# Splitting the second token group's operand straight from the transposed input, with the norm's roots applied as panels leave PSUM, and one ring of raw buffers

## The chip, the cores and the metric

The kernel runs on one core of a Trainium2 chip. The metric is device microseconds of one execution; of the kernel before there are three timed runs, and their median is the time to beat. Beside them stands one profiled execution, from which every duration comes. The engines are PE (TensorE, matmul), ACT (ScalarE), DVE (VectorE), POOL (GpSimd) and SP (SyncE, which here issues most loads).

## The reference, cut to what matters

One layer of a streaming encoder: 1024 prompt frames and 128 sample frames (8 streams of 16), each of 2048 channels, all in f32.

```
h = x * rsqrt(mean(x*x, -1) + eps) * norm_pre
q_sb,k_sb,v_sb,gate_sb,q_r,k_r,v_r,gate_r = split(h @ w_in)       # 8 panels of 8 heads x 128
o_sb = stick_breaking(q_sb, k_sb, v_sb)      # prompt: causal; samples: over 1024 cached keys and values
o_r, state = retention(rope(q_r), rope(k_r), v_r)                  # chunks of 64
y = concat(head_rms(o_sb) * g * silu(gate_sb), head_rms(o_r) * g * silu(gate_r))
out = x + rms_norm(y @ w_out) * norm_post
```

The number that the change moves is the **root**, `rsqrt(mean(x*x) + eps)`, one per token. It is a factor of a whole row of `h`, so it can be multiplied into `x` ahead of the projection or into the panel `h @ w_in` behind it.

## The kernel before, in words

Tokens are worked in two groups. **Group 0** holds tiles 0 to 3 of the prompt and the sample tile (640 tokens, moved as pieces of 256 and 384); **group 1** holds tiles 4 to 7 (512 tokens, one piece). f32 products are made of three reduced ones: each operand is split into a high and a low part (ACT copies the high part, DVE subtracts: `split`, L165 to L168), and PE does high·high, high·low and low·high.

**The moving operand** of a group is `h` transposed, 16 blocks of 128 channels, kept as four quarters of four blocks (`mh`, `ml`). There is one such buffer, so group 1's quarter q overwrites group 0's.

**A panel** (`project`, L394) is 128 columns of `w_in`: four loads of weights `wr` of 256 KB, each split into `wh`, `wl` (two buffers each) and used in a block of 24 products in group 0 (12 in group 1). **Row products** (`project_rows`, L414) give v of two heads with tokens on partitions, from weights `wrn`.

**Prologue** (L508 to L627). Group 0's operand is split from the transposed input `x_cols` with only `norm_pre` applied (ACT L577, DVE L578) and the first two panels of retention head 0 follow it. ACT makes the squares of the rows (`mean_square`, L535); PE spreads the roots over partitions (L550), and group 0's panels are multiplied by them where they leave PSUM (`rooted`, L467, on DVE). Then come the row products of v, and `stage_rest` (L594), a job that is stepped between matmuls: it loads the rows of tiles 4 to 7, squares them, loads their part of `x_cols`, multiplies it by `norm_pre` and the roots (DVE L610) and stores it to the DRAM tensor `s_h` (4 MB). The gate panel of retention head 0 is computed beside it.

**Heads.** The loop at L1086 goes over groups and heads. Per head it computes panels for retention q (column 4), k (5), gate (7), and stick-breaking q (0), k (1), gate (3); the attention work of both branches runs as jobs that emit a piece after so many matmuls (`tick`). The order listings below show in what order each engine's rows stand.

**The change of groups.** With head 7 of group 0 the last two panels (columns 7 and 3) are made together by `project_pair` (L400): blocks 7.0, 3.0, 7.1, 3.1, 7.2, 3.2, 7.3, 3.3, where 3.1 is column 3 with quarter 1. Between them `load_moving` (L244) is stepped: each step splits one block of group 1's operand out of a raw buffer `mr` (read back from `s_h`) and asks for a later one. A split of quarter q waits until PE has done block 3.q. Weights `wr` and `wrn` share a ring of five raw buffers (tag "wr"); `mr`, `kpast` (old keys, re-read per head in group 1) and the left operands of the later phases share a ring of three (tag "mr").

**After the heads**, the output projection runs as a Strassen-like set of products of sums (`left`, `left_sample`, `product`), and its raw buffers come out of the same two rings.

Of the kernel before, what the change touches and what calls it, by code (L numbers as in the profile page):

```python
# [29 lines left out]
D_REST = 8  # L30
# [30 lines left out]
MR = 3  # L61
# [27 lines left out]
def tile_hybrid_step(  # L89
# [59 lines left out]
    roots = [const.tile([P, m], F32, name=f"root{i}") for i, (_, m) in enumerate(X_PIECES[:2])]  # L149
    root_of = const.tile([P, 5], F32, name="root_of")  # L150

    NB_TOK = GROUPS[1]["n"]
    s_h = scr.tile([P, KT, NB_TOK], F32, name="s_h")
# [10 lines left out]
    def split(hi, lo, src):  # L164
        return (  # L165
            nc.scalar.activation(hi, src, AF.Copy),  # L166
            nc.vector.tensor_tensor(lo, src, hi.bitcast(F32), ALU.subtract),  # L167
        )  # L168
# [75 lines left out]
    def load_moving(mov, at, n, src):  # L244
# [59 lines left out]
    def left(gi, n, hi, lo, bufs, tag, deep):  # L304
# [3 lines left out]
        def load(h):  # L308
            r = bufs.tile([P, 256], F32, name=tag, tag=tag, bufs=deep)
# [16 lines left out]
    def left_sample(kk, hi, lo, bufs, tag, deep):  # L326
        raw = []

        def load(h):
            r = bufs.tile([P, P], F32, name=tag, tag=tag, bufs=deep)  # L330
            pin(nc.sync.dma_start(r, s_y[0][kk * H + h][:, 4 * P : 5 * P]))
            raw.append(r)
# [81 lines left out]
    def project_rows(g, mov, col, dst, off, loads=None):  # L414
# [5 lines left out]
        for w in range(KT // 2):  # L420
            wr = wp.tile([P, 2, 2 * P], F32, name="wrn", tag="wr", bufs=5)
# [22 lines left out]
        for b, bank in enumerate(banks):  # L444
            m = min(2, nt - 2 * b)
            if phase[0] == 0:
                for i in range(m):
                    t = 2 * b + i
                    nc.scalar.activation(
                        dst[:, off + t].rearrange("p j d -> p (j d)"), bank[:, i, :], AF.Copy,  # L450
                        scale=root_of[:, t : t + 1],
                    )
                continue
            nc.scalar.activation(
                dst[:, off + 2 * b : off + 2 * b + m].rearrange("p t j d -> p t (j d)"), bank[:, :m, :], AF.Copy
            )

    with ExitStack() as s1:
# [3 lines left out]
        def evac_split(acc, hi, lo, off=0):  # L462
            for a, (o, m) in acc:
                m = min(m, NB_TOK - o)
                split(hi[:, off + o : off + o + m], lo[:, off + o : off + o + m], a[:, :m])

        def rooted(dst, a, i, m):  # L467
            nc.vector.tensor_tensor(dst, a[:, :m], roots[i][:, :m], ALU.mult)

        def gate(acc, tag):  # L470
            e = ep.tile([P, NMAX], F32, name=tag, tag=tag)
            for i, (a, (o, m)) in enumerate(acc):
                if phase[0] == 0:
                    rooted(e[:, o : o + m], a, i, m)
                    s = ep.tile([P, 512], F32, name="sw", tag="sw", bufs=1)
                    nc.scalar.activation(s[:, :m], e[:, o : o + m], AF.Sigmoid)
                    nc.vector.tensor_tensor(e[:, o : o + m], e[:, o : o + m], s[:, :m], ALU.mult)
                    continue
                nc.scalar.activation(e[:, o : o + m], a[:, :m], AF.Sigmoid)
                nc.vector.tensor_tensor(e[:, o : o + m], e[:, o : o + m], a[:, :m], ALU.mult)  # L480
# [17 lines left out]
        def ret_values(g, mov, h, loads=None):  # L498
            pair["r"] = ep.tile([P, 5, 2, P], F32, name="rv", tag="rv")
            project_rows(g, mov, col(6, h), pair["r"], 0, loads)  # L500
# [9 lines left out]
        with tc.tile_pool(name="p0", bufs=2) as p0, tc.tile_pool(name="p0s", bufs=1) as p0s, tc.tile_pool(  # L510
# [6 lines left out]
            pre = p0s.tile([P, KT], F32, name="pre")  # L517
            nc.sync.dma_start(pre, pre_cols)

            def load_x(t):  # L520
                halves = []
                for c in range(2):
                    xt = p0.tile([P, HALF], F32, name="xt", tag="xc0", bufs=4)
                    nc.sync.dma_start(xt, x_rows(t)[:, c * HALF : (c + 1) * HALF])
                    halves.append(xt)
                return halves

            def load_cols(piece, k, m):
                o, n = X_PIECES[piece]
                xc = p0.tile([P, m, n], F32, name=f"xc{piece}", tag=f"xc{piece % 2}", bufs=4)  # L530
# [4 lines left out]
            def mean_square(xt, ssq, i):  # L535
                for c, half in enumerate(xt):
                    pin(nc.scalar.activation(half, half, AF.Square, accum_out=ssq[:, c, i : i + 1]))
# [15 lines left out]
            def second_panel(w):  # L553
                wr = wp.tile([P, WQ, P], F32, name="wr", tag="wr", bufs=5)
# [16 lines left out]
            for piece, (o, m) in enumerate(X_PIECES[:2]):  # L571
                for w in range(KT // WQ):
                    xc = xcs[piece][w]
                    for j in range(WQ):
                        k = w * WQ + j
                        hi, lo = (half[w][:, j, o : o + m] for half in mov)
                        nc.scalar.activation(hi, xc[:, j, :], AF.Copy, scale=pre[:, k : k + 1])  # L577
                        nc.vector.scalar_tensor_tensor(  # L578
                            lo, xc[:, j, :], pre[:, k : k + 1], hi.bitcast(F32), ALU.mult, ALU.subtract
                        )  # L580
# [3 lines left out]
            ssq5 = p0s.tile([P, 2, len(tiles)], F32, name="ssq5")  # L584
            for i, t in enumerate(tiles):
                mean_square(load_x(t), ssq5, i)
# [7 lines left out]
            def stage_rest():  # L594
                rest = GROUPS[1]["tiles"]
                ssq = p0s.tile([P, 2, len(rest)], F32, name="ssq4")
                for i, t in enumerate(rest):
                    xt = load_x(t)
                    yield 6
                    mean_square(xt, ssq, i)  # L600
                    yield 4
                rb = p0s.tile([P, NB_TOK], F32, name="rb4")
                spread(rb, rows_of(ssq, "p4"), 0, last)
                yield 4
                for w in range(KT // 2):
                    xc = load_cols(2, 2 * w, 2)
                    yield 6
                    for j in range(2):
                        k = 2 * w + j
                        nc.vector.scalar_tensor_tensor(  # L610
                            xc[:, j, :], xc[:, j, :], pre[:, k : k + 1], rb, ALU.mult, ALU.mult
                        )
                        yield 4
# [3 lines left out]
            rstd = rows_of(ssq5, "p5")  # L617
            nc.vector.tensor_copy(root_of, rstd)
            for root, at in zip(roots, (0, 2)):
                spread(root, rstd, at, last)  # L620
            for table in (*first, *ropes):
                for i, (o, m) in enumerate(X_PIECES[:2]):
                    rooted(table[:, o : o + m], table[:, o : o + m], i, m)
# [970 lines left out]
```

## Time and profile before

| what | us |
|---|---|
| three timed runs: median (lowest to highest) | 2292.41 (2291.46 to 2292.89) |
| the profiled execution | 2297.38 |
| its span, in which every position below is counted | 2295.4 |
| PE busy in it | 2245.6 |
| DVE busy | 1254.0 |
| ACT busy | 918.2 |
| PE idle in it (span less busy) | 49.8 |

How to read it: the profile groups instructions by source line. "out<-in" names the tile written and the tile read; behind it stand the shape, the count, the busy time, the mean of one in ns, and the idle time of that engine just before such rows with what ended it. "PEclk" is the granted TensorE clock as a share of full speed. PE is busy nearly all the time, so the question is always where its few idle stretches lie, and at which clock it runs behind them.

### The profile page before, as it was taken

Reading aid. Unit: us, or ns where it says so; the run is one execution under the profiler, and the core shown is the slowest. Engines: PE = TensorE matmul, PEld = TensorE weight load, DVE = VectorE, ACT = ScalarE, POOL = GpSimd, SP = SyncE. Lnnn points to the kernel's source line nnn. Section 1 sums busy time; section 2 is a strip of 40 time slices with the busy share of each in tenths; the row PEclk is TensorE's granted clock in tenths of the full one; section 3 lists DMA queues with packets and bytes.
Section 4 is the critical chain, followed back from the end, with each engine's and each line's share of the span. In section 5 each row is a group of like instructions: output and inputs, shape, how many; then the busy total and the mean of one; then the engine's idle time right before and its main releaser. Section 6 shows DMA issues by size and latency. Waiting matters only on the chain.

```text
span 2295.4 us, 38963 instructions
## 1 busy us (share of the span) xinstructions
PE 2245.6 (98%) x14306; PEld 2028.6 (88%) x14306; DVE 1254.0 (55%) x2587; ACT 918.2 (40%) x1945; POOL 339.5 (15%) x577
## 2 busy tenths in 40 slices
PE   7899999999999999999999999999999999999998
PEld 7899999999999999998888889898889987888886
DVE  5435444454545545355556565656565567556567
ACT  7333333333333333334333333343443444545363
POOL 0002020110202020111202111120212212000020
PEclk9999999999999999999999999999999999999999
DMA  8947656675557648568669778788887767766586
GB/s 293 329 141 188 194 177 190 181 211 173 161 178 201 201 154 233 168 189 263 186 201 234 220 212 234 218 230 218 229 218 218 218 166 195 248 210 186 143 223 175
DMA packets 442848, 470.99 MB, mean 205 GB/s; under 512 B 182560, under 2 KB 302368, under 8 KB 442144
## 3 DMA queue, kind: packets, MB, share of 16 engines
q1 hardware_dynamic: 319408, 304.09, 46.8%
q0 software_dynamic: 28720, 78.41, 12.2%
q10 hardware_dynamic: 94528, 86.00, 11.8%
q8 instruction: 112, 1.84, 0.3%
q14 instruction: 80, 0.66, 0.1%
HBM read 363.51 MB, written 114.29 MB: 208 GB/s over the span
## 4 chain that ended last, share of the span: by engine, by line
PE 88%; DMA 6%; DVE 2%; ACT 2%; issue 1%; SPq 1%; DVEq 0%; ACTq 0%
PE acc L380 47%; PE accn L436 16%; PE a L1228 5%; PE a L1227 5%; PE a L1224 5%; PE pa L796 2%; PE z L766 2%; PE zc L835 1%; PE pd L899 1%; DMA ro<-s_rk 1%; DMA mr<-s_h 1%; DMA s_rk<-rk 1%; PE pa L944 1%; PE pS L959 1%; PE pa L949 1%
## 5 line engine op out<-in xcount | busy, mean ns | idle before, releaser
L380 PE MATMUL acc<-mh,wh 128*128 128x256 f32 (+2 forms) x2304 | 668.0, 341 | 7.3 <-ACT wh L166 7.3
L380 PE MATMUL acc<-mh,wl 128*128 128x256 f32 (+2 forms) x2304 | 660.6, 339 | 3.9 <-DVE wl L167 3.9
L380 PE MATMUL acc<-ml,wh 128*128 128x256 f32 (+2 forms) x2304 | 663.3, 340 | 0.0
L167 DVE TENSOR_TENSOR wl<-wr,wh 128x512 fp32r<-128x512 f32 x504 | 345.9, 689 | 418.9 <-ACT wh L166 396.6
L166 ACT ACTIVATE wh<-wr 128x512 fp32r<-128x512 f32 x504 | 317.0, 631 | 639.1 <-PE acc L380 336.9
L380 PEld LDWEIGHTS acc<-mh,wh 128*128 128x128 f32 x2304 | 422.0, 189 | 39.4 <-ACT wh L166 7.3
L380 PEld LDWEIGHTS acc<-mh,wl 128*128 128x128 f32 x2304 | 426.4, 189 | 32.1 <-DVE wl L167 4.4
L380 PEld LDWEIGHTS acc<-ml,wh 128*128 128x128 f32 x2304 | 423.8, 189 | 31.6 <-issue 3.3
L436 PE MATMUL accn<-whn,mh 128*128 128x256 f32 x1152 | 330.1, 287 | 7.6 <-ACT whn L166 7.6
L436 PE MATMUL accn<-wln,mh 128*128 128x256 f32 x1152 | 328.5, 285 | 0.0
L436 PE MATMUL accn<-whn,ml 128*128 128x256 f32 x1152 | 328.3, 285 | 0.0
L436 PEld LDWEIGHTS accn<-whn,mh 128*128 128x128 f32 x1152 | 222.6, 194 | 10.6 <-ACT whn L166 8.1
L436 PEld LDWEIGHTS accn<-wln,mh 128*128 128x128 f32 x1152 | 223.2, 194 | 1.1 <-issue 0.2
L436 PEld LDWEIGHTS accn<-whn,ml 128*128 128x128 f32 x1152 | 223.0, 194 | 0.0
L166 ACT ACTIVATE whn<-wrn 128x512 fp32r<-128x512 f32 x128 | 80.6, 633 | 186.2 <-PE accn L436 88.7
L167 DVE TENSOR_TENSOR wln<-wrn,whn 128x512 fp32r<-128x512 f32 x128 | 87.5, 686 | 118.8 <-ACT whn L166 115.0
L659 POOL DMA_DIRECT2D be<-s_be x128 | 94.3, 743 | 145.9 <-DMA s_be<-be 126.2
L695 DVE TENSOR_TENSOR_SCAN kp<-kp 128x1152 f32<-128x1152 f32 (+4 forms) x40 | 82.7, 2067 | 52.1 <-POOL kp L684 35.4
L822 POOL DMA_DIRECT2D kcT<-cache_k x64 | 34.8, 547 | 448.6 <-PE pd L899 268.1
L684 POOL TENSOR_SCALAR_AFFINE_SELECT kb<-kb 128x128 f32<-128x128 f32 x64 | 30.1, 479 | 454.2 <-ACT kb L678 452.1
L1228 PE MATMUL a<-wh,ml 128*128 128x512 f32 x240 | 93.6, 390 | 0.0
L1227 PE MATMUL a<-wl,mh 128*128 128x512 f32 x240 | 93.4, 389 | 0.0
(283 smaller groups left out, 2954.1 us busy)
## 6 DMA issues: line engine op xcount, KB each, us to landing
wr<-w_cols SPq DMA_DIRECT2D x384, 256.0 KB, 4.5
wrn<-w_rows SPq DMA_DIRECT2D x128, 256.0 KB, 3.8
kcT<-cache_k POOLq DMA_DIRECT2D x64, 512.0 KB, 8.1
vc<-cache_v SPq DMA_DIRECT2D x64, 512.0 KB, 5.9
wr<-s_b SPq DMA_DIRECT2D x80, 256.0 KB, 4.1
br<-w_out SPq DMA_DIRECT2D x64, 256.0 KB, 5.1
s_b<-br ACTq DMA_DIRECT2D x32, 512.0 KB, 5.6
wr<-w_out SPq DMA_DIRECT2D x48, 256.0 KB, 3.7
```

Source lines behind the costliest of these rows:

```text
L166: nc.scalar.activation(hi, src, AF.Copy),
L167: nc.vector.tensor_tensor(lo, src, hi.bitcast(F32), ALU.subtract),
L380: last = nc.tensor.matmul(a[:, :m], lhs[:, j, :], rhs[w][:, j, o : o + m], start=(w == 0 and j == 0 and n == 0), stop=(w == KT // WQ - 1 a ...
L436: anchor[0] = nc.tensor.matmul(a, lhs[q][:, jj, ts], rhs[:, j, :], start=(w == 0 and j == 0 and n == 0 and t % 2 == 0), stop=(w == KT // 2 ...
L659: q.dma_start(raw[32 * i : 32 * i + 32, :].rearrange("p (k a) -> p k a", a=32), s[:, :, 32 * i : 32 * i + 32].rearrange("k (j b) a -> b (k ...
L695: nc.vector.tensor_tensor_scan(rev, rev, rev, 1.0, ALU.mult, ALU.bypass)
L766: nc.tensor.matmul(z[:, :c], q2[a][:, i * P : (i + 1) * P], k2[b][:, s : s + c], start=(m == 0), stop=(m == 2),)
L796: nc.tensor.matmul(po[:, :P], at[:, j, :], vn[:, j, :], start=(j == 0), stop=(j == t))
L822: ready.append((kc, nc.gpsimd.dma_start(kc, cache_k[h, m // 4, m % 4])))
L1224: ins = nc.tensor.matmul(a, hi[k][:, ts], wh, start=first, stop=False)
L1227: nc.tensor.matmul(a, hi[k][:, ts], wl, start=False, stop=False)
L1228: anchor[0] = nc.tensor.matmul(a, lo[k][:, ts], wh, start=False, stop=last)
```

## The change

1. **Prologue.** `stage_rest` and `s_h` are gone. The squares become a job `squares` that is paced behind the matmuls of the row products (group 0, pace 5) and of the gate panel (group 1, pace 4). The roots of group 0 are spread at the end of the row products (`roots_first`). The roots of group 1 are spread behind the gate panel and put in a small DRAM tensor `s_root` (256 KB), which is read back into the one table `roots` when group 1 starts.
2. **Group 1's operand** is split straight from `x_cols`, with `norm_pre` as a factor in both halves of the split (`split_pre`).
3. **Group 1's panels** are rooted where they leave PSUM, as group 0's were: gates, stick-breaking q and k, and v (ACT with a scale per tile of 128x256 in place of 128x512 per copy). RoPE tables are rooted once for the group.
4. **Buffers.** One ring of eight (tag "wr") serves `wr`, `wrn`, `mr`, `kpast` and the left operands; `mr` is asked for four ahead in place of three. `kpast` is asked for ahead of the k panel of its head.

```diff
-D_REST = 8
+D_X = (5, 4)
-MR = 3
+RAW = 8
+MR = 4
...
+    def split_pre(hi, lo, src, k):
+        nc.scalar.activation(hi, src, AF.Copy, scale=pre[:, k : k + 1])
+        nc.vector.scalar_tensor_tensor(
+            lo, src, pre[:, k : k + 1], hi.bitcast(F32), ALU.mult, ALU.subtract
+        )
...
-            r = wp.tile([P, n], F32, name="mr", tag="mr", bufs=MR)
+            r = wp.tile([P, n], F32, name="mr", tag="wr", bufs=RAW)
...
-            split(hi[q][:, j, at : at + n], lo[q][:, j, at : at + n], raw.pop(0))
+            split_pre(hi[q][:, j, at : at + n], lo[q][:, j, at : at + n], raw.pop(0), k)
...
-            wr = wp.tile([P, WQ, P], F32, name="wr", tag="wr", bufs=5)
+            wr = wp.tile([P, WQ, P], F32, name="wr", tag="wr", bufs=RAW)
...
         def gate(acc, tag):
-            for i, (a, (o, m)) in enumerate(acc):
-                if phase[0] == 0:
-                    rooted(e[:, o : o + m], a, i, m)
...
-                nc.scalar.activation(e[:, o : o + m], a[:, :m], AF.Sigmoid)
-                nc.vector.tensor_tensor(e[:, o : o + m], e[:, o : o + m], a[:, :m], ALU.mult)
+            for a, (o, m) in acc:
+                rooted(e[:, o : o + m], a, o, m)
+                s = ep.tile([P, 512], F32, name="sw", tag="sw", bufs=1)
+                nc.scalar.activation(s[:, :m], e[:, o : o + m], AF.Sigmoid)
+                nc.vector.tensor_tensor(e[:, o : o + m], e[:, o : o + m], s[:, :m], ALU.mult)
...
-            def stage_rest():
-                rest = GROUPS[1]["tiles"]
...
-                    for j in range(2):
-                        k = 2 * w + j
-                        nc.vector.scalar_tensor_tensor(
-                            xc[:, j, :], xc[:, j, :], pre[:, k : k + 1], rb, ALU.mult, ALU.mult
-                        )
-                        yield 4
-                    nc.scalar.dma_start(s_h[:, 2 * w : 2 * w + 2, :], xc)
...
+            job = Job(squares(tiles, ssq[0], D_X[0]))
+            tick()
+
+            def roots_first():
+                drain(job)
+                nc.vector.tensor_copy(root_of[:, : len(tiles)], rows_of(ssq[0], "p5"))
+                for o, m in X_PIECES[:2]:
+                    spread(roots[:, o : o + m], root_of, o // P, last)
+
+            ret_values(g0, mov, 0, None, roots_first)
+            rooted_tables((*first, *ropes), X_PIECES[:2])
+            job = Job(squares(GROUPS[1]["tiles"], ssq[1], D_X[1]))
+            tick()
             first = *first, pair["r"][:, :, 0, :], dict(rg=gate(project(g0, mov, col(7, 0)), "rg"))
             drain(job)
+            nc.vector.tensor_copy(root_of[:, len(tiles) :], rows_of(ssq[1], "p4"))
+            rb = p0s.tile([P, NB_TOK], F32, name="rb4")
+            spread(rb, root_of, len(tiles), last)
+            nc.scalar.dma_start(s_root, rb)
...
-        from_h = lambda k: s_h[:, k, :]
+        def from_h(k):
+            o, n = X_PIECES[2]
+            return x_cols[:, KT * o + k * n : KT * o + (k + 1) * n]
...
+                    if gi == 1:
+                        kp = wp.tile([P, NB_TOK], F32, name="kpast", tag="wr", bufs=RAW)
+                        nc.sync.dma_start(kp, s_k[h])
                     acc = held or project(g, mov, col(1, h))
...
-                        if gi:
-                            nc.scalar.activation(kT[:, o : o + m], a[:, :m], AF.Copy)
-                        else:
-                            rooted(kT[:, o : o + m], a, i, m)
...
+                    for a, (o, m) in acc:
+                        rooted(kT[:, o : o + m], a, o, m)
```

**Where rows move.** On ACT in the prologue, between the two first panels and the row products, this stands before (`sw` belongs to the rotation of q and k, `xt` rows are squares, `whn` are the row products' weights):

```order
L487 ACTIVATE sw<-acc_200 64x384
L488 ACTIVATE sw<-acc_200 64x384
L537 ACTIVATE xt,ssq_523<-xt 128x1024 x4
L487 ACTIVATE sw<-acc_201 64x256
L488 ACTIVATE sw<-acc_201 64x256
L166 ACTIVATE whn<-wrn 128x512
L537 ACTIVATE xt,ssq_523<-xt 128x1024
```

Of the changed kernel, the same place on ACT:

```order
L489 ACTIVATE sw<-acc_199 64x384
L490 ACTIVATE sw<-acc_199 64x384
L168 ACTIVATE whn<-wrn 128x512
L489 ACTIVATE sw<-acc_200 64x256
L490 ACTIVATE sw<-acc_200 64x256
L168 ACTIVATE whn<-wrn 128x512 x3
L542 ACTIVATE xt,ssq_555<-xt 128x1024
```

The first `whn` stands ahead of every square now, and three more of them ahead of the first square.

At the change of groups, ACT has this before (`mh_12031` is quarter 0 of group 1's operand; the three `wh` rows split the weights of blocks 3.1, 7.2 and 3.2):

```order
L166 ACTIVATE wh<-wr 128x512
L716 ACTIVATE sq,ssq_11536<-ro 128x128
L166 ACTIVATE mh_12031<-mr 128x512 x3
L166 ACTIVATE wh<-wr 128x512
L166 ACTIVATE mh_12031<-mr 128x512
L733 DMA s_y_6_144<-sg 128x128
L952 ACTIVATE ro<-pa 128x128
L716 ACTIVATE sq,ssq_11536<-ro 128x128
L166 ACTIVATE wh<-wr 128x512
```

Of the changed kernel there, where `mh_11994`, `mh_12092` and `mh_12201` are quarters 0 to 2:

```order
L173 ACTIVATE mh_11994<-mr,pre 128x512 x4
L168 ACTIVATE wh<-wr 128x512
L940 ACTIVATE ro<-pa 128x128
L168 ACTIVATE wh<-wr 128x512
...
L173 ACTIVATE mh_12092<-mr,pre 128x512 x4
L168 ACTIVATE wh<-wr 128x512
L666 ACTIVATE kp<-zc 128x512
L168 ACTIVATE wh<-wr 128x512
L667 ACTIVATE be<-zc 128x512
L173 ACTIVATE mh_12201<-mr,pre 128x512 x4
```

All four splits of a quarter now stand ahead of the weights of block 3.1, 3.2 or 3.3 (the `wh` directly behind them).

SP, which issues the loads, has this at that place before:

```order
L369 DMA wr<-w_cols 128x512 x5
L505 DMA cosT<-c_cos 128x512
L369 DMA wr<-w_cols 128x512
L506 DMA sinT<-c_sin 128x512
L422 DMA wrn<-w_rows 128x512
L659 DMA do<-s_o_6_1_0_11784 32x4x32 x4
L422 DMA wrn<-w_rows 128x512 x2
L250 DMA mr<-s_h 128x512 x3
```

Of the changed kernel, with the loads of 3.0 and 7.1 in the first row, of 3.1 and 7.2 in the sixth, of 3.2 and 7.3 in the last:

```order
L377 DMA wr<-w_cols 128x512 x2
L258 DMA mr<-x_cols 128x512 x2
L507 DMA cosT<-c_cos 128x512
L508 DMA sinT<-c_sin 128x512
L258 DMA mr<-x_cols 128x512 x2
L647 DMA do<-s_o_6_1_0_11745 32x4x32 x4
L377 DMA wr<-w_cols 128x512 x2
L258 DMA mr<-x_cols 128x512 x2
L909 DMA dT<-c_dt 128x256
L922 DMA S<-s_S_98 128x128
L258 DMA mr<-x_cols 128x512 x2
L377 DMA wr<-w_cols 128x512 x2
```

Before, all of the pair's weights are asked for ahead of the raw blocks `mr`; now the two alternate in one ring.

More of the change, by code (lines that the diff above doesn't have):

```diff
@@ L148, in tile_hybrid_step @@
     gains = const.tile([P, 2, H], F32, name="gains")
-    roots = [const.tile([P, m], F32, name=f"root{i}") for i, (_, m) in enumerate(X_PIECES[:2])]
-    root_of = const.tile([P, 5], F32, name="root_of")
+    pre = const.tile([P, KT], F32, name="pre")
+    roots = const.tile([P, NMAX], F32, name="roots")
+    root_of = const.tile([P, NT], F32, name="root_of")
     NB_TOK = GROUPS[1]["n"]
-    s_h = scr.tile([P, KT, NB_TOK], F32, name="s_h")
+    s_root = scr.tile([P, NB_TOK], F32, name="s_root")
     s_k = [scr.tile([P, NB_TOK], F32, name=f"s_k{h}") for h in range(H)]
@@ L533, in load_cols, with squares, load @@
                 return xc
[L535 to L537 removed]
+            def squares(tiles, ssq, pace):
+                todo = [(i, t, c) for i, t in enumerate(tiles) for c in range(2)]
+                raw = []
+                def load(i, t, c):
+                    xt = p0.tile([P, HALF], F32, name="xt", tag="xc0", bufs=4)
+                    nc.sync.dma_start(xt, x_rows(t)[:, c * HALF : (c + 1) * HALF])
+                    raw.append(xt)
+                for item in todo[:4]:
+                    load(*item)
+                yield pace
+                for n, (i, t, c) in enumerate(todo):
+                    xt = raw.pop(0)
+                    pin(nc.scalar.activation(xt, xt, AF.Square, accum_out=ssq[:, c, i : i + 1]))
+                    if n + 4 < len(todo):
+                        load(*todo[n + 4])
+                    yield pace
             def rows_of(ssq, name):
@@ L616, in tile_hybrid_step @@
-            first = [rope(list(zip(acc, g0["pieces"])), tag, *ropes) for acc, tag in zip(accs, ("rq", "rk"))]
[L617 to L623, printed above, removed]
-            job = Job(stage_rest(), D_REST)
@@ L1101, in ret_queries @@
                         loads = None
+                        nc.sync.dma_start(roots[:, :NB_TOK], s_root)
+                        rooted_tables(ropes, g["pieces"])
                     acc = project(g, mov, col(4, h))
```

118 lines of the change are left out of this document (39 added, 79 removed).

## The prediction

> **What bounds the kernel now.** I read the page's first part, then the list of all waits of PE, then the timeline around each.
>
> ```profile
> PE 2245.6 (98%) x14306; PEld 2028.6 (88%) x14306; DVE 1254.0 (55%) x2587; ACT 918.2 (40%) x1945; POOL 339.5 (15%) x577
> ```
>
> PE is the bound. It idles 2295.4 − 2245.6 = 49.8 us, and the matmuls stay the same in number and shape but for a few small ones. So a change can take away only idle time and slow clock, or add them. The waits of PE over the whole span (line waited for, total, times, longest):
>
> ```profile
> PE accn L436 <- ACT whn L166: 7.6, 2, 4.7
> PE acc L380 <- ACT wh L166: 7.3, 1, 7.3
> PE pSs L1024 <- ACT kb L679: 5.0, 1, 5.0
> PE pa L944 <- DVE so L799: 4.3, 3, 2.0
> PE acc L380 <- DVE wl L167: 3.9, 1, 3.9
> PE pa L796 <- DVE kp L756: 3.8, 4, 1.1
> PE pS L959 <- DVE rkn L1049: 3.1, 3, 1.6
> ```
>
> The two L436 waits and the `wl` one belong to the prologue, the `pSs` one to the change of groups, the others but the start's 7.3 to the heads. The change reaches all three places.
>
> **The prologue: a gain.** Three waits of PE stand there, in its timeline (start, duration, ..., idle before):
>
> ```profile
> 43.46 0.80 PE L436 MATMUL accn<-whn,mh 128*128 128x256 f32 x2 [4.74 <-ACT whn L166]
> ...
> 67.92 1.01 PE L436 MATMUL accn<-whn,mh 128*128 128x256 f32 x3 [2.85 <-ACT whn L166]
> ...
> 101.21 0.50 PE L380 MATMUL acc<-mh,wl 128*128 128x256 f32 x1 [3.89 <-DVE wl L167]
> ```
>
> Behind each the clock is low. The windows (length, then PE busy, and PEclk after POOL's):
>
> ```profile
> 44.00:50.00 6.00, 6.00 (x42) 5.98 (x41) 3.03 (x7) 5.93 (x13) 0.00 (x0) 0.77 0.95 324
> ...
> 68.00:75.00 7.00, 7.00 (x36) 6.99 (x37) 3.10 (x12) 1.46 (x3) 0.00 (x0) 0.57 0.89 295
> ...
> 101.00:107.00 6.00, 5.79 (x29) 5.79 (x30) 4.06 (x13) 3.90 (x6) 3.37 (x6) 0.72 0.84 249
> ```
>
> Lost to the clock are 6 × 0.23 = 1.4, 7 × 0.43 = 3.0 and 6 × 0.28 = 1.7 us. With the idle time the three places cost 6.1, 5.9 and 5.6, together 17.6 us.
>
> The first wait is four squares ahead of the first weights on ACT:
>
> ```profile
> 37.70 1.06 ACT L537 ACTIVATE xt<-xt 128x1024 f32<-128x1024 f32 x1
> ...
> 40.83 1.04 ACT L537 ACTIVATE xt<-xt 128x1024 f32<-128x1024 f32 x1
> ...
> 42.78 0.63 ACT L166 ACTIVATE whn<-wrn 128x512 fp32r<-128x512 f32 x1
> ```
>
> In the new order `whn` follows the `sw` rows that end at 37.70, so it is done at about 38.3, ahead of the panels' end at 43.46 − 4.74 = 38.72. `wln` needs 0.69 on DVE behind it. What is late next is that `wln` or the load: up to 0.8 us of wait, which I take. The second wait comes from squares and `wrn` loads mixed with 18 `xt` loads on ACT and SP; in the new order the row weights are asked for behind only four `xt` and the later squares stand behind weights, so I take it as gone. The third is DVE in `stage_rest`:
>
> ```profile
> 99.14 1.41 DVE L610 SCALAR_TENSOR_TENSOR xc<-xc,pre,rb 128x512 f32<-128x512 f32 x2 [3.86 <-DMA xc<-x_cols]
> 100.47 1.91 DVE L167 TENSOR_TENSOR wl<-wr,wh 128x512 fp32r<-128x512 f32 x3
> ```
>
> The multiplication waits 3.86 us for its load, and `wl` for the next panel is queued behind it. Both the 16 multiplications (11 us of DVE) and the 8.4 MB written to and read from `s_h` go; the split's load comes from the input with the same 256 KB per block, and `s_root` adds 0.5 MB. New there: the spread of the roots now ends the row products and waits for the last squares. Row products follow each other by 0.12 us at full clock:
>
> ```profile
> 82.01 0.28 PE L436 MATMUL accn<-whn,ml 128*128 128x256 f32 x1
> 82.13 0.28 PE L436 MATMUL accn<-whn,mh 128*128 128x256 f32 x1
> ```
>
> Ten squares of about 1.04 us lie beside 240 of them, 29 us, which covers them; if their loads are late, PE waits as long as the second wait before, with its clock 5.9. Gain: 17.6 − 0.8 = about 17; bounds 17 − 5.9 = 11 and 17.6.
>
> **The change of groups: a loss.** Before, PE has one wait there, behind ACT:
>
> ```profile
> 1084.23 0.19 ACT L716 ACTIVATION_READ_ACCUMULATOR sq<-ro 128x1 f32 x1
> 1087.95 0.63 ACT L166 ACTIVATE mh<-mr 128x512 fp32r<-128x512 f32 x1 [3.53 <-DMA mr<-s_h]
> 1088.48 0.47 ACT L678 ACTIVATE kb<-z 128x384 f32<-128x384 f32 x1
> 1088.85 0.48 ACT L679 ACTIVATE kb<-z 128x384 f32<-128x384 f32 x1
> ```
>
> ```profile
> 1077.00:1100.00 23.00, 18.04 (x138) 15.62 (x138) 13.27 (x30) 10.15 (x21) 4.94 (x9) 0.85 0.76 247
> ```
>
> The clock in this window costs 18.0 × 0.15 = 2.7 us at most, of which I take 2.2; with the 5.0 idle this wait costs 7.2 us. It should go, since the last raw blocks are asked for earlier. What comes in its place is worked out from the ring. Eight slots are given out in the order mr0 to mr3, 7.0, 3.0, 7.1, mr4 to mr7, 3.1, 7.2, mr8 to mr11, 3.2, 7.3, mr12 to mr15, 3.3. So 3.1 takes the slot of mr3, 3.2 that of mr6, 3.3 that of mr10. These are raw blocks that can be split only when PE has done block 3.0, 3.1 or 3.2: **the weights of a block wait for a split that waits for the block two before it.** Before, the weights had their own five slots. The prices, from ACT, DVE and SP of before:
>
> ```profile
> 1054.47 0.63 ACT L166 ACTIVATE wh<-wr 128x512 fp32r<-128x512 f32 x1 [0.37 <-PE acc L380]
> ...
> 1055.30 1.66 ACT L166 ACTIVATE mh<-mr 128x512 fp32r<-128x512 f32 x3
> 1058.15 0.63 ACT L166 ACTIVATE wh<-wr 128x512 fp32r<-128x512 f32 x1 [1.19 <-PE acc L380]
> ...
> 1062.35 0.63 ACT L166 ACTIVATE wh<-wr 128x512 fp32r<-128x512 f32 x1 [0.26 <-PE acc L380]
> ```
>
> ```profile
> 1055.95 1.90 DVE L167 TENSOR_TENSOR ml<-mr,mh 128x512 fp32r<-128x512 f32 x3
> ```
>
> ```profile
> 1048.79 4.50 SPq L659 DMA_DIRECT2D do<-s_o  x4
> ```
>
> ```profile
> wr<-w_cols SPq DMA_DIRECT2D x384, 256.0 KB, 4.5
> wrn<-w_rows SPq DMA_DIRECT2D x128, 256.0 KB, 3.8
> ```
>
> The `wh` rows start when PE frees a buffer, so block 3.0 ends at 1054.5, 7.1 at 1058.2, 3.1 at 1062.4. In the new kernel four `mh` (0.55 each) and four `ml` (0.63 each) follow 3.0: mr3 is free at about 1058.1. On SP the load of 3.1 stands behind two more `mr`, which wait for mr1 and mr2, and behind the four `do` (0.4 to 1.1 each): issue at about 1060.0, landing 4.5 later, `wh` 0.6 later, 1065.1. PE wants it at 1058.2: 6.9 us idle. By the same steps: 3.2 needs the third split after 3.1 and has no `do` ahead, 4.0 late, of which some 1.8 are filled by score products (`z`, `zc`) that now stand there in PE's order, so 2.2; 3.3 likewise 4.5 less 0.9, so 3.6. Each wait has a slow clock behind it; for the three I take 2.2, 1 and 1.7 (the losses above being 1.4 to 3.0). Sum 12.7 + 4.9 = 17.6, less the 7.2 that go: **+10**. Bounds: if SP's `do` cost nothing and the loads land in the 3.8 us of the row weights, each wait is one or two us shorter and the two small ones keep the clock: +4; if the fillers are late and each wait costs its clock in full (3.0), +20.
>
> [...]
>
> **Group 1's heads: a small loss.** DVE gets a multiplication of 128x512 for each of 16 gates, 8 q and 8 k, at the 0.69 us of a row of this size (L167), 22 us; ACT loses 8 copies of k (0.59 each) and makes v in 16 + 16 pieces in place of 8 + 8.
>
> ```profile
> L167 DVE TENSOR_TENSOR wl<-wr,wh 128x512 fp32r<-128x512 f32 x504 | 345.9, 689 | 418.9 <-ACT wh L166 396.6
> ```
>
> ```profile
> 1100.00:1950.00 850.00, 837.92 (x4772) 727.95 (x4771) 511.54 (x965) 340.20 (x714) 151.58 (x239) 1.00 0.78 213
> ```
>
> DVE is 60% busy in that stretch and becomes 63%, so weights are still split in time: the cover is a panel's block of products that runs while the next is prepared. Without it, what shows is latency: 32 × 0.69 = 22. PE's waits for DVE there come to 4.3 + 3.8 + 3.1 = 11.2 us; growing with DVE's load (4%) they add 0.5, and if a third of the rows lengthen a wait, 7. I take +2, with −2 (`kpast` is loaded and split earlier) and +7 as ends. The last phases share the ring too; PE is busy in all of it there,
>
> ```profile
> 2000.00:2250.00 250.00, 250.00 (x1105) 207.01 (x1103) 150.60 (x315) 123.19 (x275) 17.32 (x20) 1.00 0.68 193
> ```
>
> and no slot waits for a late split, so 0, with 2 either way. Group 0's heads: the same rows, 0.
>
> **Sum.** −17 + 10 + 2 = −5 us. Of the profiled execution, 2297.4 (the span and 2 around it), that makes 2292; the median of the runs is 5.0 lower, so the forecast is **2287.4**.
>
> **The rivals.** (a) *The ring does not bite.* If the loads of 3.1 to 3.3 get their slots in time (the raw blocks are split sooner than I think), the three waits shrink to 8 us with their clock, and the old 7 are gone too: −17 + 2 − 7 + 8 = −14, 2278. For it: PE's job rows can fill. Against: the split of a quarter cannot precede block 3.q. (b) *The ring bites in full, slower.* At the change of groups each of the three blocks waits a whole chain of split, issue, load and split, 6.9 + 4.0 + 4.5 with 3.0 of clock each, 24, and the old wait stays (the 7.2 are not gained): −17 + 24 + 2 = +9, 2301; it turns the sum's sign once that place costs over 15 us net. For it: the loads stand on one SP queue in order, and 4.50 us for four `do`. (c) *The prologue gains only half.* The squares' loads (9.4 MB at the 295 to 324 GB/s of the windows is 30 us) keep the roots, and so PE, waiting: −9 + 10 + 2 = +3, 2295. That the change doesn't do what it says is in here: the row products would still wait for squares.
>
> **How the numbers follow.** Forecast 0.42, (a) 0.20, (b) 0.22, (c) 0.16. A measurement here can tell about 0.2%, 4.6 us, from no change: faster means below 2287.8, slower above 2297.0. The forecast lies at that edge: 0.24 faster, 0.18 same. (a) is faster; (b) slower 0.19, same 0.03; (c) same 0.11, slower 0.05. Faster 0.44, same 0.32, slower 0.24. The range takes in (a), (c) and (b) with 2 to 3 us around them, 2275 to 2303; what it leaves out is the corner in which every cost falls on its upper bound at once (−11 + 20 + 7 = +16, 2308). The forecast's own range is 2282 to 2293.
>
> **What would show it.** Right: no wait over 1 us on `accn` in the first 100 us, and the q panel behind the gate panel starting near 85 and not 101.2; at the change of groups three waits of `acc` for `wh` of some 7, 2 and 4 us, with `wr` as what ACT waited for, and no `pSs` wait of 5. Wrong: a wait of `pb` for `dg` in the prologue (c), one wait at most there (a), or waits of over 5 us at all three blocks (b); in the heads, DVE waits of PE over 20 us in place of 11.

## The result: slower, and where the time went

The changed kernel took 2313.57 us (median of 4 runs, 2311.38 to 2317.64), against 2292.0 for the kernel before (a fourth run is in that median). The ratio is 1.0096, 95% interval 1.0078 to 1.0113: 22 us **slower**, where 5 us faster was forecast and 2303 was the end of the range.

First the same views as before. The changed kernel's engines:

```profile
PE 2254.2 (98%) x14306; PEld 2026.5 (88%) x14306; DVE 1262.0 (55%) x2606; ACT 921.8 (40%) x1953; POOL 344.6 (15%) x577
```

Its span is 2309.7 us, so PE idles 55.5 us (49.8 before) and is busy 8.6 us longer with the same number of matmuls. The clock explains little of that: the mean granted clock over the span is 0.993 in both traces, so what the prologue won of it (1.00 over the first 100 us, 0.94 over the first 117 before) was lost again behind new waits (0.95 over the 102.9 us of the last pair, 1.00 there before). The rest of the 8.6 us stays open. The waits of PE (line waited for, total, times, longest):

```profile
PE acc L388 <- ACT wh L168: 14.3, 4, 6.8
PE pa L784 <- DVE kp L744: 12.0, 7, 4.5
PE a L1211 <- ACT wh L168: 7.2, 4, 3.8
PE pS L947 <- DVE rkn L1037: 5.4, 4, 3.2
PE pb L558 <- DVE dg L556: 1.4, 1, 1.4
PE accn L447 <- DVE wln L169: 0.8, 1, 0.8
```

The `whn` and `wl` waits of the prologue and the `pSs` wait of the change of groups are gone. In their place stand more waits for `kp` and `rkn` (the heads of group 1), and for `wh` both in panels and in the products of the output projection (L1211). The 6.8 in the first line is the start's wait, 7.3 before.

Totals do not say where. PE does the same panels and products in the same order, so I took the start of the same matmul in both traces and subtracted. In us, at nine places named by their time in the kernel before (minus is earlier):

```
place (us, before)         466   1050   1124   1257   1379   1493   1890   1980    end
changed kernel           -19.3  -18.4  -17.2  -15.5  -10.4   -3.4   -3.1   +9.8  +14.3
```

So the prologue gained 19; group 0's heads lost 1, the change of groups (1050 to 1124) another 1; group 1's heads (1124 to 1890) lost 14, most of it in two of them (1257 to 1379 and 1379 to 1493, 5 and 7); the last pair of panels and the first products behind it (1890 to 1980) lost 13; the output projection 4.5. These positions come from profiled executions. Those of the kernel before took 2297.4 and, a second time, 2298.0, about 5 us over the median of its timed runs, while that of the changed kernel took 2311.4, 2 below its median. So positions show where, and the ratios of timed runs show how much; the sums differ by some 7 us.

**The prologue** went as forecast. PE's timeline of the changed kernel behind the gate panel:

```profile
85.80 0.71 PE L558 MATMUL pb<-dg,ones 128*128 128x128 f32 x4 [1.39 <-DVE dg L556]
86.27 0.42 PE L388 MATMUL acc<-mh,wh 128*128 128x384 f32 x1
```

The panel that began at 101.21 begins about 86, and only two short waits are left.

**The last pair of panels.** Of the changed kernel, first what SP waited for in 1870 to 1975, then its timeline:

```profile
SPq L647 <- DMA s_rk<-rk: 27.3, 1, 27.3
```

```profile
1902.14 0.30 SPq L647 DMA_DIRECT2D ro<-s_rk  x1
1902.53 3.34 SPq L339 DMA_DIRECT2D wr<-s_y  x6
1905.92 2.10 SPq L647 DMA_DIRECT2D ro<-s_rk  x3
1908.13 0.99 SPq L377 DMA_DIRECT2D wr<-w_cols  x2
```

SP stands 27 us at one read (`ro<-s_rk`), for the store of rk to land; behind it stand six raw blocks of a left operand (`s_y`) and, behind those, weights for the panels that PE is about to make. Of ACT and of PE there:

```profile
1906.48 0.31 ACT L168 ACTIVATE mh<-wr 128x128 fp32r<-128x128 f32 x1 [6.52 <-DMA wr<-s_y]
...
1912.49 1.34 ACT L168 ACTIVATE wh<-wr 128x512 fp32r<-128x512 f32 x2 [2.60 <-DMA wr<-w_cols]
```

```profile
PE a L1211 <- ACT wh L168: 5.0, 2, 3.8
PE acc L388 <- ACT wh L168: 3.3, 1, 3.3
```

PE waits for weights that came late (window 1890 to 1975, total, times, longest), with a lower clock behind them (the last number but two):

```profile
1913.00:1975.00 62.00, 56.09 (x253) 45.20 (x254) 36.46 (x82) 29.79 (x72) 8.33 (x12) 0.92 0.68 179
```

The whole stretch, before and changed (length, PE busy):

```profile
1890.00:1980.00 90.00, 87.09 (x426) 72.67 (x425) 58.32 (x114) 46.63 (x107) 19.57 (x30) 1.00 0.71 195
```

```profile
1886.90:1989.80 102.90, 93.49 (x426) 75.80 (x425) 59.71 (x117) 47.32 (x110) 23.40 (x30) 0.95 0.66 183
```

Of the 12.9 us, 6.5 are idle time of PE (9.4 against 2.9), and a clock of 0.95 over 102.9 us is worth some 5 more.

**A head of group 1.** DVE of the changed kernel near 1468:

```profile
1467.46 0.71 DVE L1033 STREAM_TRANSPOSE rkn<-ro 128x512 f32<-128x512 f32 x1 [4.29 <-DMA wr<-w_cols]
1468.10 1.20 DVE L744 STREAM_TRANSPOSE kp<-be 128x1024 f32<-128x1024 f32 x1
```

and in the same head of the kernel before:

```profile
1472.77 1.24 DVE L756 STREAM_TRANSPOSE kp<-be 128x1024 f32<-128x1024 f32 x1
1473.93 0.67 DVE L1045 STREAM_TRANSPOSE rkn<-ro 128x512 f32<-128x512 f32 x1
```

The two rows have changed places. Both wait for a round trip through DRAM: `rkn` for rk (stored, read back as `ro`), `kp` for `be`. PE wants `kp`: of the 12.0 us that it waits for `kp`, 4.5 stand here. The profile puts the wait of `rkn` down to a load of weights, but by their own records the last read of `ro` landed at 1467.38, just before the row starts. The last read of `be` landed late too, at 1466.1. POOL, which issues it, and its time to landing (the last number):

```profile
1458.49 0.79 POOL L647 DMA_DIRECT2D be<-s_be  x1 [4.24 <-issue]
```

```profile
be<-s_be POOLq DMA_DIRECT2D x1, 128.0 KB, 7.6
```

So `kp` stood 2.0 us (1466.1 to 1468.1) behind `rkn`; the rest of its delay is the late read. In the kernel before, the last read of `be` landed at 1469.0, 3.7 us ahead of its row.

### The profile page after: what moved, and what is told of

Its sections match the earlier page's. It is cut to its first block, busy times and chain, and to the rows that moved or that the text cites. A ratio compares the mean times of both kernels' runs of the same rounds, so it can differ in the third digit from the quotient of the medians.

```text
span 2309.7 us, 38917 instructions
## 1 busy us (share of the span) xinstructions
PE 2254.2 (98%) x14306; PEld 2026.5 (88%) x14306; DVE 1262.0 (55%) x2606; ACT 921.8 (40%) x1953; POOL 344.6 (15%) x577
## 4 chain that ended last, share of the span: by engine, by line
PE 85%; DMA 7%; DVE 3%; ACT 2%; issue 2%; SPq 1%; POOL 0%; DVEq 0%; ACTq 0%; POOLq 0%
PE acc L388 45%; PE accn L447 17%; PE a L1214 4%; PE a L1211 4%; PE a L1215 4%; PE pa L784 2%; PE z L754 2%; PE zc L823 1%; PE pd L887 1%; DMA wr<-w_cols 1%; DMA s_rk<-rk 1%; DMA ro<-s_rk 1%; DMA wr<-w_out 1%; PE pa L932 1%; PE pS L947 1%
## 5 line engine op out<-in xcount | busy, mean ns | idle before, releaser
L1211 PE MATMUL a<-wh,mh 128*128 128x512 f32 x240 | 93.7, 395 | 7.2 <-ACT wh L168 7.2
```

Source lines behind the costliest of these rows:

```text
L1211: ins = nc.tensor.matmul(a, hi[k][:, ts], wh, start=first, stop=False)
```

## The experiments

Three theories of the loss. **Ring**: sharing the raw buffers does it, and of that, either the change of groups or the left operands. **Roots**: the 32 extra DVE rows lengthen the chains in group 1's heads. **Order**: the emitted order and the loads in flight have shifted, so that a round trip through DRAM now stands in front of something that PE wants (the expectations call this lanes, too, and loaded queues where the round trip itself is late). Kernel 1 is that of experiment 1, and so on. Ratios are against the kernel before on the same chip. Positions are of one profiled execution each.

### 1. Two rings again

```diff
-RAW = 8
-MR = 4
+RAW = 5
+MR = 3
-            r = wp.tile([P, n], F32, name="mr", tag="wr", bufs=RAW)
+            r = wp.tile([P, n], F32, name="mr", tag="mr", bufs=MR)
...
-            yield from left(0, 5, *mine[0, 5], wp, "wr", MR)
+            yield from left(0, 5, *mine[0, 5], wp, "mr", MR)
...
-                        kp = wp.tile([P, NB_TOK], F32, name="kpast", tag="wr", bufs=RAW)
+                        kp = wp.tile([P, NB_TOK], F32, name="kpast", tag="mr", bufs=MR)
...
```

> The changed kernel, but with the two rings of the kernel before: five raw buffers for wr and wrn, three for mr, kpast and the left operands. All else stays changed. Theory ring: the prologue keeps its 18 us, and what is lost behind it (about 12 us in the heads of group 1, 13 in the last pair of panels, 4 in the output projection, 2 at the change of groups) comes back but for a few us: about 2274 to 2280. Theory roots (the extra DVE rows lengthen the chains of group 1's heads): the 12 us of the heads stay, only the last pair comes back: about 2290 to 2296. Theory lanes (which DMAs wait for each other by accident moved, and any change of order moves them): anything between, with waits at other places than in the changed kernel.

Measured: 2286.65 us, ratio 0.9967 (0.9955 to 0.9979), 7.6 us **faster** than before and some 30 faster than the changed kernel. The ring brings the loss: undoing it returns all of it and more. The last pair comes back (−11.0 at 1890, −12.3 at 1980). About 6 us of the prologue's gain are still lost between 1050 and 1379, so the time lies above the ring theory's interval and below that of roots.

### 2. The ring alone, on the kernel before

```diff
-MR = 3
+RAW = 8
+MR = 4
...
-            wr = wp.tile([P, WQ, P], F32, name="wr", tag="wr", bufs=5)
+            wr = wp.tile([P, WQ, P], F32, name="wr", tag="wr", bufs=RAW)
...
-            yield from left(0, 5, *mine[0, 5], wp, "mr", MR)
+            yield from left(0, 5, *mine[0, 5], wp, "wr", MR)
...
```

> The kernel before with one thing changed: one ring of eight raw buffers for wr, wrn, mr, kpast and the left operands, four mr asked for ahead. Prologue, s_h and roots as before. Theory ring: slower than before by the loss seen behind the prologue, 20 to 35 us, 2312 to 2327, with the SP queue held some 27 us by the read of s_rk in the last pair. Theory roots: only the last pair is lost, 13 to 17 us, 2305 to 2309, and the waits of PE for DVE in the heads stay at 11 us in sum.

Measured: 2309.2 us, ratio 1.0070 (1.0056 to 1.0085), 16 us slower. By position it loses 11 us in the last pair (−2.6 at 1890, +8.5 at 1980), nothing at the change of groups (−2.8 to −2.9) and nothing in the heads (−2.9 to −2.6). So the ring costs the last pair by itself; the loss in the heads needs the rest of the change too. The time lies below the ring theory's interval and 0.2 above that of roots, and the loss stands where roots expected it; kernels 3 and 4 decide between the two.

### 3 and 4. Without the roots on DVE, with one ring and with two

```diff
             for a, (o, m) in acc:
+                if phase[0]:
+                    nc.scalar.activation(e[:, o : o + m], a[:, :m], AF.Sigmoid)
+                    nc.vector.tensor_tensor(e[:, o : o + m], e[:, o : o + m], a[:, :m], ALU.mult)
+                    continue
                 rooted(e[:, o : o + m], a, o, m)
...
+                        if gi:
+                            split(q2[0][:, o : o + m], q2[1][:, o : o + m], a[:, :m])
+                            continue
...
+                        if gi:
+                            nc.scalar.activation(kT[:, o : o + m], a[:, :m], AF.Copy)
+                            continue
```

> The changed kernel without the DVE multiplications by the roots in group 1's gates, q and k (left out: those roots; the forms of the kernel before stand there). One ring of eight stays. Theory roots: 12 us of the heads come back, about 2301. Theory ring: at most 3 us come back, 2310 to 2314, and the last pair and the heads lose as in the changed kernel.

> Two rings as before, and group 1's gates, q and k without the DVE multiplications by the roots (left out: those roots). Prologue and operand split stay changed. Theory roots: the heads of group 1 give back what the two-ring kernel still lost there, 7 to 10 us, so 2277 to 2280. Theory lanes and order: the waits of PE in the heads move to other places but stay near 18 us in sum, 2283 to 2287.

Measured: with one ring 2307.62 us, 1.0059 (1.0045 to 1.0073); with two, 2285.71, 0.9972 (0.9962 to 0.9982). The clean pair is that with two rings: 0.9972 without the roots, 0.9967 with them. **The 22 us of DVE rows cost nothing that timed runs can tell** with two rings (the intervals exclude more than some 2.5 us), and the theory of roots falls as a cause by itself. In the one profiled execution of each the heads took 8 us less without them (−17.1 at 1124 and −19.6 at 1890, against −16.2 and −11.0); the timed runs do not bear that out, so positions of single executions can differ by that much there. With one ring 8 us come back by the ratios, more than the ring theory allowed and less than roots expected, yet not in the heads (from 1124 to 1890 the kernel without roots loses 12.6 us by position, the changed one 14.1). Where those 8 us lie stays open.

### 5. SP freed of the read that held it

```diff
-            turn_in(s, raw, nc.sync)
+            turn_in(s, raw, nc.gpsimd if gi and h == H - 1 else nc.sync)
```

> The changed kernel, with one edit: the read of s_rk of group 1's last head is issued by GpSimd and no more by SP. One ring of eight stays. Theory held queue (SP stands 27 us at that read with the weights and the left operands of the last pair behind it): the last pair gives back about 10 of its 13 us, 2300 to 2305, and the waits of acc for wh near 1913 and of a for wh near 1941 shrink below 1 us. Theory slots (the weights of the last pair wait for the left operands' slots, whoever issues): no change, 2310 to 2315, and SP waits for the split of a left operand in place of the read.

Measured: 2311.06 us, ratio 1.0078 (1.0059 to 1.0098). The interval overlaps that of the changed kernel, so no gain is shown. What SP waited for in 1865 to 1975 is now:

```profile
SPq L1228 <- DVE ml L169: 14.4, 6, 4.7
SPq L339 <- DVE wl L169: 13.1, 5, 4.7
SPq L377 <- DVE wl L169: 11.9, 4, 3.7
```

The 27 us are gone, and SP waits as long in sum (76.6 us in 1870 to 1975, 75.1 in the changed kernel), now mostly for slots: a load of a left operand (L339) for the split of a weight, a load of weights (L1228) for the split of a left operand (`ml`). The held queue was the sight that caught the eye; most of the loss does not come from it. From 1890 to 1980 the kernel still loses 11.5 us, where the changed kernel loses 12.9.

### 6. The kernel before, a second profile

> The kernel before, unchanged, for a second profile of it: its first profiled execution was 5 us above the median of the timed runs. 2290 to 2297; every theory expects the same waits of PE, about 50 us idle in sum.

Measured: ratio 0.9996 (0.9985 to 1.0006). Its positions lie within 2 us of those of the first profile, so for the kernel before the positions repeat; each of the other kernels has one profile.

### 7. Raw blocks of the change of groups apart

```diff
-RAW = 8
-MR = 4
+RAW = 5
+MR = 3
-            r = wp.tile([P, n], F32, name="mr", tag="wr", bufs=RAW)
+            r = wp.tile([P, n], F32, name="mr", tag="mr", bufs=MR)
```

> The changed kernel with the raw blocks of load_moving in three buffers of their own; weights, kpast and left operands share a ring of five. Theory slots at the change of groups: the wait for wh there (3.5 us and its slow clock) goes, the pSs wait of 5 comes back, so no more than 2 us either way from that place. The last pair still shares its ring, now of five: held queue or slots, it loses 13 or more there. So 2296 to 2312, between the two-ring kernel and the changed one; if it comes to 2287 the last pair's loss is not due to the shared ring.

Measured: 2301.09 us, ratio 1.0033 (1.0020 to 1.0045). Until 1890 it keeps all of the prologue's gain (−18.6), the heads included; then the last pair takes 16.5 us (−2.1 at 1980), with these waits of PE in 1875 to 1965:

```profile
PE a L1211 <- ACT wh L168: 7.5, 3, 5.0
PE acc L388 <- ACT wh L168: 3.4, 3, 2.7
```

Kernel 1 differs from it only in that the left operands and `kpast` stand in the other ring, with `mr`, and it gains 1.3 in that stretch. `kpast` is not loaded there, so the **left operands in the weights' ring** cost the last pair, 15 us by the ratios of kernels 7 and 1 and some 18 by position.

### 8. Left operands apart, the rest in a ring of six

```diff
-RAW = 8
+RAW = 6
...
-            yield from left(0, 5, *mine[0, 5], wp, "wr", MR)
+            yield from left(0, 5, *mine[0, 5], wp, "mr", MR)
...
```

> The changed kernel with the left operands of the last pair and the output projection in four small buffers of their own; weights, mr and kpast share a ring of six (the memory allows no more). Theory left operands (their slots in the ring cost the last pair and the projection some 15 us, the change of groups costs little): 2288 to 2298, the last pair as in the kernel before, and what remains is in the heads. Theory change of groups (the ring is dear there, as forecast, and dearer with six slots): 2300 to 2312 with waits of acc for wh of 5 us and more near 1050 to 1065.

The left operands have four buffers of their own here. Measured: 2291.93 us, ratio 0.9987 (0.9977 to 0.9998). In the last pair 0.8 us is lost (−2.5 at 1890, −1.7 at 1980), and in 1890 to 1975 no wait of PE for `wh` in a panel or a product is left there:

```profile
PE pS L947 <- DVE rkn L1037: 1.7, 1, 1.7
PE pa L932 <- DVE ro L941: 1.2, 1, 1.2
PE a L1214 <- DVE wl L169: 0.2, 1, 0.2
```

The change of groups, with only six slots, costs 2.3 us by position (−17.5 at 1050, −15.2 at 1124) and has no wait for `wh` above 0.84 us: the theory that the ring is dear there falls. What this kernel still loses, it loses in group 1's heads, 12.7 us (−15.2 to −2.5), with these waits of PE in 1110 to 1400:

```profile
PE pS L947 <- DVE rkn L1037: 5.6, 2, 3.3
PE pa L932 <- DVE so L787: 3.4, 1, 3.4
PE pa L784 <- DVE kp L744: 0.8, 1, 0.8
```

Again it is `rkn`, near 1154 and 1256; the changed kernel's longest wait for it is near 1254.

### 9 and 10. The turn of rk emitted later

```diff
-            yield D_TI[phase[0]]
+            yield (32, 22)[phase[0]]
             tied(nc.vector.transpose(rkn.rearrange("p k d -> p (k d)")[:, : nt * P], raw))
```

> The changed kernel with one number changed: the turn of rk in group 1 (the DVE transpose of what was read back from s_rk) is emitted 22 matmul steps behind the read and no more 13, so that in the head near 1467 it stands behind the transpose of kp again, as in the kernel before. Theory order on DVE: that head's loss of 6 us goes, the one near 1250 stays, 2304 to 2309. Theory loaded queues (the round trip itself is late): the turn still comes late and PE waits for rkn instead, 2309 to 2315.

> Two rings as before and the late turn. Theory order on DVE: the 5 us that the two-ring kernel loses near 1252 go, 2280 to 2284, faster than both kernels. Theory loaded queues: no change, 2285 to 2289.

Measured, with one ring: 2306.62 us, ratio 1.0055 (1.0041 to 1.0069), 9 us better than the changed kernel. DVE in the head that lost 7 us:

```profile
1461.52 1.24 DVE L744 STREAM_TRANSPOSE kp<-be 128x1024 f32<-128x1024 f32 x1
1462.68 0.67 DVE L1033 STREAM_TRANSPOSE rkn<-ro 128x512 f32<-128x512 f32 x1
```

`kp` is in front again, neither row waits, and by position the kernel loses 0.7 us from 1379 to 1493 in place of 7.0. This is what the theory of order expected, but it does not show the order alone to be that loss: the reads came earlier here as well, that of `be` at 1461.1 in place of 1466.1.

With two rings: 2286.3 us, 0.9968 (0.9957 to 0.9980), the same as kernel 1, as loaded queues expected; the 2280 to 2284 of order was wrong. Kernel 1 has the cleaner sight of the order, in the head near 1250:

```profile
1250.46 0.71 DVE L1033 STREAM_TRANSPOSE rkn<-ro 128x512 f32<-128x512 f32 x1 [2.63 <-DMA ro<-s_rk]
1251.10 1.20 DVE L744 STREAM_TRANSPOSE kp<-be 128x1024 f32<-128x1024 f32 x1
```

There the last read of `be` had landed at 1246.65, DVE stood idle for 2.63 us with `kp` behind `rkn` though its reads were in, and PE waited 2.7 us for `kp`. The later turn did not put `kp` in front in that head (in kernel 10 `rkn` starts at 1248.69, `kp` at 1249.50), but its read landed at 1248.27 and `rkn` did not wait. By position kernel 10 loses 1.0 us from 1124 to 1379 and kernel 1 loses 6.1; the timed runs show no difference.

## Why the prediction was wrong, step by step

**What bounds the kernel**: right. PE is busy 98% of the span in both traces (2254.2 of 2309.7 us, 2245.6 of 2295.4).

**Prologue, −17, bounds −11 to −17.6**: right, 19 by position at 466, a little over the bound, and 17 to 18 in the kernels with two rings. (The ring of eight alone has 3 of it: −3.4 in kernel 2.)

**Change of groups, +10, bounds +4 to +20**: the chain is there, but its size is wrong; the place cost 1, and 0 to 2.3 in the other kernels with that ring. From the start of block 7.1 to that of block 3.3 the changed kernel takes 29.06 us, before 19.07:

```profile
1036.15:1065.21 29.06, 24.86 (x165) 20.88 (x164) 15.10 (x29) 13.59 (x28) 5.16 (x10) 0.97 0.76 248
```

```profile
1054.51:1073.58 19.07, 19.07 (x134) 19.07 (x134) 12.44 (x24) 10.70 (x24) 4.08 (x8) 1.00 0.78 241
```

That is 10 us more, of which 4.2 are idle; the 5.8 more of busy time hold work that PE did later before (165 matmuls against 134). The 7.2 of the old `pSs` wait are saved. In place of the forecast's 17.6 for the new waits and their clock stand 4.2 idle and some 2.4 of clock (0.93 over the 35 us from 1065). My chain was too long at its head. SP, ACT and DVE of the changed kernel:

```profile
1029.10 2.83 SPq L647 DMA_DIRECT2D do<-s_o  x4
1038.16 1.01 SPq L377 DMA_DIRECT2D wr<-w_cols  x2
```

```profile
1036.64 2.55 ACT L173 ACTIVATE mh<-mr,pre 128x512 fp32r<-128x512 f32 x4
1041.31 0.63 ACT L168 ACTIVATE wh<-wr 128x512 fp32r<-128x512 f32 x1 [2.12 <-DMA wr<-w_cols]
```

```profile
1037.38 2.74 DVE L174 SCALAR_TENSOR_TENSOR ml<-mr,pre,mh 128x512 fp32r<-128x512 f32 x4 [1.08 <-ACT mh L173]
```

I had put the load of 3.1 behind the fourth split and behind the four `do`. The `do` had gone out 9 us before, the load went out 1.5 us after the splits began, and it landed in 3.1 us, not 4.5. It went out as the first of the four `ml` ended (1038.13). Those of 3.2 and 3.3, at 1048.65 and 1058.15, also went out as the first `ml` of the next four ended. So each took the slot of the first raw block of its quarter, not of the fourth, third and third, as I had counted: the times fit slots that come back in the order in which they are released, not in the order in which they were given out. The load of 3.3 then took 6.3 us to land, and it is the one that PE noticed. PE waited 0.67 us at 3.1, none at 3.2 and 3.53 at 3.3, where 6.9, 2.2 and 3.6 stood in the forecast.

**Heads of group 1, +2, bounds −2 to +7**: wrong, 14 by position. I priced the rows that are added (nothing that shows, kernels 3 and 4), and neither the order in which the rows then stand nor the round trips through DRAM that some of them wait for. In the head near 1468 the reads came late and `rkn` stood ahead of `kp`; the order accounts for 2.0 us of it directly, and kernel 9, which loses nothing there, changed both. The other heads are not settled: the waits for the round trips of rk and `be` move from head to head between kernels. Near 1250 the store of rk took 9.6 us to land in the changed kernel (median us to landing is the last number), where it took 3.4 in kernel 7; in the first it was issued behind three weight loads and three reads of `be` of the 5 us before, which themselves took 7.5 to 10 us. Of the changed kernel, then of kernel 7:

```profile
s_rk<-rk ACTq DMA_DIRECT2D x1, 256.0 KB, 9.6
```

```profile
s_rk<-rk ACTq DMA_DIRECT2D x1, 256.0 KB, 3.4
```

That the deeper ring bunches weight loads ahead of it is argued from these times, not shown. For it: by position the heads (1124 to 1890) lose 6.5 to 14 us in every changed kernel with a ring of six or eight, and between −2.5 and +5 in those whose weights have five raw buffers, kernel 7 with its shared ring among them. Against it: kernel 2 has eight and no loss in the heads. No run varies the depth alone.

**Last phases, 0, "no slot waits for a late split"**: this is the step that failed most, 13 us in the last pair and 4.5 in the projection. I looked at where PE was 100% busy (2000 to 2250) and not at 1890 to 1980, where first the left operands and the last panels' weights alternate in one ring, just as `mr` and weights do at the change of groups. The same chain that I priced there stood here a second time: a slot is free only when the block that held it has been split, and those splits are paced by PE's progress. Kernels 1, 2, 7 and 8 agree that the left operands in the weights' ring cost the last pair; of the chain itself the traces show SP's waits for splits (14.4, 13.1 and 11.9 us in kernel 5). The 4.5 us of the projection are not tied to the ring: kernel 2 loses 0.9 there and kernel 1, with two rings, 2.8.

**The rivals.** (b), the ring in full, came nearest in sign and size (2301), by luck: it was to decide at the change of groups, and its waits do not stand there. (c) did not occur, though its sign, the wait of `pb` for `dg`, is there with 1.4 us. (a) did as far as the change of groups goes, and its gain was lost behind it. My own sign for the heads, DVE waits of PE over 20 us, was not reached either: they are 18.8 in 1110 to 1960, 11.2 before.

On the clock: behind the waits of 3.28 and 3.85 us of the last pair it was 0.52 over 1913 to 1920 and 0.54 over 1940.8 to 1944.2. Behind the wait of 2.85 us in the kernel before it was 0.57 over 68 to 75. At the change of groups it was 1.00 over 1042 to 1049, behind the 0.67 us at 3.1, and 0.64 over 1065.1 to 1072, behind the 3.53 us at 3.3. That the two small waits there would keep the clock, as the lower bound had it, was my estimate: 3.2 did not wait, and behind 3.3 the clock fell.

What stays open: most of the heads' loss, the 8 us that kernel 3 won back, 4.5 us in the output projection, the part of PE's 8.6 busy us that the clock does not explain, and why profiled executions of the kernel before lie 5 us above its timed ones.

**A version that beats both**: the changed kernel with the two rings of the kernel before (kernel 1), 0.9967, or 2286.65 us.

## What to carry to other kernels

The shared ring coupled its users here: in kernel 5 loads of weights waited 14.4 us for splits of left operands, and loads of left operands 13.1 us for splits of weights, and the left operands in the weights' ring cost the last pair some 15 us (kernels 7 and 1). So keep users whose release waits on the bottleneck engine out of a ring with loads that this engine wants next. When a change merges rings, list every stretch of the program in which two users alternate, and price the chain in each, not only in the one that the change was about. Added rows on an engine with room (22 us on DVE, 55% busy) cost nothing that showed here (0.9967 with them, 0.9972 without); look at which rows changed places, and whether one that waits for a round trip through DRAM now stands ahead of one that is ready, as near 1250 in kernel 1, where DVE stood idle for 2.63 us.

## What the runs showed of the hardware

Of two 256 KB stores of rk, one landed after 3.4 us (kernel 7) and one after 9.6 (the changed kernel), where six transfers issued in the 5 us before it took 7.5 to 10 us themselves. And freeing SP of a read at which it stood 27 us brought no gain that could be measured (11.5 us lost in the last pair in place of 12.9, ratios 1.0078 and 1.0096 with overlapping intervals): SP waited for slots instead.
